# A hybrid decoder layer on one core: two groups' raw weights loaded ahead of conditioning rows, a list of thresholds for the visits, and another offset for the first parts

## The chip, the cores and the metric

The kernel runs on one core of one Trainium2 chip. The metric is the time on the device in microseconds (us); lower is better. Times given as a median come from runs without a profile; the views come from one profiled execution, which has a time of its own. TensorE multiplies matrices, VectorE and ScalarE work on elements, GpSimd is hardly used, and SyncE (SP) issues most transfers.

## The reference

One decoder layer over 256 tokens of width 2048, all in fp32. A conditioning vector c gives six vectors of 2048 values by one large product, and the first two scale and shift the normalized input. The first large product, h W_in, feeds a retention branch and an HGRN2 branch; a gated feed-forward part follows.

```python
mod = jax.nn.silu(c) @ w_ada[l] + b_ada[l]
shift1, scale1, gate1, shift2, scale2, gate2 = jnp.split(mod, 6, axis=-1)

h = modulate(rms_norm(x, g_norm1[l]), shift1, scale1)
p = h @ w_in[l]
rq, rk, rv, rg, hq, hf, hi, hg, ga, gb = jnp.split(p, split_at, axis=-1)
...
x = x + gate1[:, None, :] * (merged @ w_out[l])
h2 = modulate(rms_norm(x, g_norm2[l]), shift2, scale2)
u = causal_depthwise_conv(h2 @ w_up[l], conv_w[l], conv_b[l])
a, bgl = jnp.split(u, 2, axis=-1)
x = x + gate2[:, None, :] * ((jax.nn.silu(a) * bgl) @ w_down[l])
return rms_norm(x, g_final)
```

## The kernel before

**Products in three parts.** A product in fp32 is made of three products in a faster format: every weight and every activation is split into an upper part (rounded) and a lower part (the rest), and upper x upper, upper x lower and lower x upper are summed. For a piece of weights, `load` (line 158) brings 128 partitions x up to two k tiles x 512 columns by the SP queue into one of eleven buffers called raw; `upper` (line 169) makes the upper part wh on ScalarE (line 176); `rest` (line 179) makes the lower part wl on VectorE (line 181). `pieces` (line 185) hands out such pieces one after the other. wh and wl have four buffers each, with 64 spare elements; `part` (line 164) places the part at an offset in bytes given by `shift`, a pair for wh and wl. `COLS` is (8, 8), the default is (0, 0).

**The stage that the change touches.** It multiplies h by twelve column groups of W_in (`ATT`), each 512 columns wide, over sixteen k tiles of 128 rows. Groups are counted from 0, so the sixth and seventh are groups 5 and 6. Groups 0 to 3 give their output turned (`mm_cols`, twelve matmuls of 256 columns a k tile, lines 221, 222 and 225), groups 4 to 11 in rows (`mm_rows`, six matmuls of 512 columns a k tile, lines 205, 206 and 210). In the column groups the weights are the stationary operand.

A k tile of h needs its own scale and shift, that is two dot products of c's silu with two rows of w_ada a k tile. Each row comes in two loads, and VectorE multiplies and sums each of the four (`ada_dot`, line 507); ScalarE turns the sums into scale and shift (lines 518, 519 and 524) and makes h's upper part and h itself (lines 434 and 435), and VectorE h's lower part (line 436). So the k tiles of h come one after the other, and the stage works on those that are there. Rows of w_ada and pieces of weights share the raw buffers and the SP queue.

The first two k tiles are worked off by hand for groups 0 to 3 (lines 899 to 948), in an order that is kept as written (`pin`). Line 949 prepares the first piece of group 4 (`FIRST`), lines 950 and 951 start the conditioning of the third k tile: its first two loads and products. From line 952 on the order on an engine is the scheduler's, which places instructions by the order of the program and by when it expects their inputs.

**Visits.** `visits` (line 971) plans the rest: it goes round the groups, and at each visit a group takes all k tiles that have come into use since its last one. `work` counts the k tiles done over all groups and begins at 8; the number of k tiles in use is have = min(16, 2 + int((work - LAG) / ADA_EVERY)), with LAG 2 and ADA_EVERY 11. A visit finishes the conditioning that it needs (line 1003), multiplies into a PSUM bank (`products`), prepares the next visit's first piece (`early`, line 986) and then adds the bank to the group's sum in SBUF (`take`, line 876: a copy on ScalarE, line 880, at a group's first visit; an add on VectorE, line 882, later). The banks called pg are two, so a visit starts when the take of the visit two before is done; groups 0 and 1 stay in banks of their own until the end. After each piece `pump` lets the conditioning go on by a share of `pace`, about 0.73 a pair of k tiles where one of its steps counts 1.15.

The plan has 56 visits and 105 pieces. Its first visits are, as (group, k tiles): (4, 2), (5, 2), (6, 2), (7, 3), (8, 3), (9, 3), (10, 3), (11, 4), (0, 2), (1, 2), (2, 2), (3, 3); the last are (5, 3), (6, 3), (7, 2), (8, 2), (9, 2), (10, 1), (11, 1). Behind the groups follow the keys of the retention, the gates, the two output products, the up projection and the down projection, which the change does not touch. Groups 0, 2 and 4, when complete, start the HGRN2 work of four heads (`hgrn`, line 610), whose element-wise steps fill VectorE and ScalarE beside the products.

Of the kernel before, what the change touches and what calls it, by code (L numbers as in the profile page):

```python
# [23 lines left out]
KT = D // P  # L24
# [5 lines left out]
G = 512  # L30
NORM_EPS = 1e-6
HEAD_EPS = 1e-5
FIRST = 4
RESIDENT = 2
ADA_EVERY = 11
LAG = 2
NOSYNC = mybir.DependencyInfo(mybir.DependencyClass.NoSync, mybir.DependencyReason.DATA)
SMALL = 70
COLS = (8, 8)
# [21 lines left out]
class Kernel:  # L61
# [104 lines left out]
        full = self.wp.tile([P, 2 * G + 64], F32R, name=f"{name}_{self.n}", tag=name, bufs=4)  # L166
        return full[:, shift // 4 : shift // 4 + m * w].rearrange("p (m w) -> p m w", m=m)

    def upper(self, src, m, w, gain=None, shift=(0, 0)):

        raw = self.load(src, m, w)
        if gain is not None:
            self.pin(self.nc.vector.tensor_tensor(raw, raw, gain[:, None, :].to_broadcast([P, m, w]), ALU.mult))
        self.n += 1
        wh, wl = [self.part(n, m, w, at) for n, at in zip(("wh", "wl"), shift)]
        self.pin(self.nc.scalar.activation(wh, raw, AF.Copy))  # L176
        return raw, wh, wl
# [4 lines left out]
        self.pin(self.last)  # L182
        return wh, wl

    def pieces(self, src, kts, gain=None, shift=(0, 0)):

        uppers = []
        for k in range(0, kts, 2):
            m = min(2, kts - k)

            while len(uppers) <= k // 2 + (gain is not None) and 2 * len(uppers) < kts:
                at = 2 * len(uppers)
                z = min(2, kts - at)
                uppers.append(self.upper(src[:, at : at + z, :], z, G, gain, shift))
            wh, wl = self.rest(uppers[k // 2])
            uppers[k // 2] = None
            yield [(k + j, wh[:, j, :], wl[:, j, :]) for j in range(m)]
# [35 lines left out]
    def mm_apart(self, pss, pieces, act):  # L233

        nc = self.nc
        n = range(len(pss))
        for pick, cols in ((0, slice(0, T)), (0, slice(T, 2 * T)), (1, slice(0, T))):
            for i in n:
                for j in range(4):
                    out = pss[i][j // 2][:, j % 2 * T : (j % 2 + 1) * T]  # L240
                    w = pieces[i][pick][:, 0, j * P : (j + 1) * P]
                    self.pin(nc.tensor.matmul(out, lhsT=w, rhs=act[:, cols], start=False, stop=False, skip_group_check=True))
# [17 lines left out]
    def wide_group(self, src, act):  # L260

        nc = self.nc
        pgs = [self.pg(), self.pg()]
        ps = pgs[0][:2] + pgs[1][:2]
        steps = list(range(0, KT, 4))
        pieces = self.pieces(src, KT, shift=WIDE)
        for k in steps:
            items = [(act(kt), wh, wl) for _ in range(2) for kt, wh, wl in next(pieces)]
            for pair in (0, 2):
                self.mm_wide(ps, items, k == 0, k == steps[-1], pair)  # L270
                self.pump()
        out = self.blk([P, 4, T], name="p")
        for pair in (0, 2):
            dst = out[:, pair : pair + 2, :]
            z = pgs[pair // 2][2]
            nc.scalar.activation(dst, z[:, :, T:], AF.Copy)
            nc.vector.tensor_tensor(dst, dst, z[:, :, :T], ALU.add)
        return out
# [567 lines left out]
    def run(self):  # L846
        nc, a = self.nc, self.a
# [11 lines left out]
        def act(k):  # L859
            return hT[k // 2][:, k % 2, :]  # L860
# [32 lines left out]
        def opening(k):  # L893

            z = self.s1([P, T], name="z")
            self.pin(nc.scalar.activation(z, self.xT[0][:, k, :], AF.Identity, bias=self.dots[:, 0:1], scale=s1[:, k : k + 1]))
            return z
# [10 lines left out]
        z = opening(0)  # L908
# [9 lines left out]
        uppers = []  # L918
        for g in range(RESIDENT, FIRST):
            if g == RESIDENT:  # L920
                self.pin(nc.scalar.activation(hi, h, AF.Copy))
            uppers.append(self.upper(a["wa"][g][:, 0:1, :], 1, G))
        self.pin(nc.vector.tensor_tensor(lo, h, hi.bitcast(F32), ALU.subtract))
        rests = [self.rest(z) for z in uppers]
        self.times(1, 1, rx_sb)
# [3 lines left out]
        for g in range(RESIDENT, FIRST):  # L929
            ps[g] = self.pg()  # L930
            wh, wl = rests[g - RESIDENT]
# [3 lines left out]
        z = opening(1)  # L935
        for _ in gen:
            pass
        uppers = [self.upper(a["wa"][g][:, 1:2, :], 1, G) for g in range(RESIDENT)]
        hi, lo = act(1)[:, :T], act(1)[:, T:]
        summed(hi, z, self.dots)  # L940
        h = self.s1([P, T], name="h")
# [2 lines left out]
        rests = [self.rest(z) for z in uppers]  # L944
        self.mm_apart([ps[g] for g in range(RESIDENT)], rests, act(1))
        for g in range(RESIDENT, FIRST):
            wh, wl = self.rest(self.upper(a["wa"][g][:, 1:2, :], 1, G))
            mms[g](ps[g], [(act(1), wh[:, 0, :], wl[:, 0, :])], False, True)
        begun = list(self.pieces(a["wa"][FIRST][:, 0:2, :], 2))
        for _ in range(2):  # L950
            next(ada[2])
        self.ordered = False
# [9 lines left out]
        def visit(g):  # L962
            return COLS if g in cols else (0, 0)
# [6 lines left out]
        def visits():  # L970
            work, g = sum(done), FIRST
            seen = list(done)
            while min(seen) < KT:
                have = min(KT, 2 + int((work - LAG) / ADA_EVERY))
                m = have - seen[g]
                if m > 0:
                    yield g, m, work
                    seen[g] = have
                    work += m
                else:  # L980
                    work += 0.5
                g = (g + 1) % len(ATT)
                if have == KT and seen[0] < KT:
                    g = min(i for i in range(len(ATT)) if seen[i] < KT)

        def early(g, m):
            k = done[g]
            pieces = self.pieces(a["wa"][g][:, k : k + m, :], m, shift=visit(g))
            return chain([next(pieces)], pieces)

        small = False
        plan = list(visits())
        for g in range(RESIDENT, FIRST):
            take(g, ps[g], True)
        for n, (g, m, work) in enumerate(plan):
            if work > SMALL and not small:
                small = True
                self.small_loads(nc.sync, ("freq", "lbT", "lmask"))
                self.start(self.trig())
                self.start(self.lower_bound())  # L1000
            fresh = done[g] == 0
            have = done[g] + m
            self.finish(*ada[:have])
            bank = ps[g] if g < RESIDENT else self.pg()
            whole = g >= RESIDENT
            self.products(mms[g], bank, a["wa"][g], act, done[g], m, first=whole, last=whole or have == KT, shift=visit(g), begun=begun)
            done[g] = have
            begun = early(*plan[n + 1][:2]) if n + 1 < len(plan) else None
            if whole or have == KT:
                take(g, bank, fresh or not whole)  # L1010
            if have == KT and ATT[g] in GATES:
                nc.scalar.activation(accs[g], accs[g], AF.Silu)
                gates[GATES.index(ATT[g])] = accs[g]
            for hb in range(2):
                gs = [hb, 2 + hb, 4 + hb]
                if g in gs and min(done[i] for i in gs) == KT:
                    self.pace(0, 14.0, 24)
                    begin(self.hgrn, hb, *(accs[i] for i in gs))
                    for i in gs:
                        accs[i] = None  # L1020
# [63 lines left out]
        for j in range(4):  # L1084
            last = j == 3
            x1.append(self.load_rows(j))
            if not last:
                g = self.row(self.gate["gate1"], j, "g1")
            if j == 2:
                g3 = self.row(self.gate["gate1"], 3, "g1")  # L1090
            elif last:
                g = g3
            ps = self.products(self.mm_rows, self.po2() if last else self.pg(), a["wout"][j], actm, 0, KT, hold=4 * last, gain=g if last else None)
            if last:
                g = None
# [302 lines left out]
```

## Time and profile before

| what | us |
|---|---|
| median of 3 runs (1504.5 to 1504.94) | 1504.68 |
| the profiled execution | 1503.57 |
| its span, first to last instruction | 1501.8 |
| TensorE busy in the span | 1485.5 |
| VectorE busy | 1210.5 |
| ScalarE busy | 839.8 |

The views count from the start of the span. A row of a timeline has the start, the length, the engine (PE is TensorE, PEld its weight loads, DVE VectorE, ACT ScalarE, SPq the SP queue), the line of the kernel, the operation, the tiles as output<-inputs, the shape and a count; in brackets stands how long the engine was idle before it and what ended that. Rows of alike instructions without a gap are merged. A matmul of 512 columns is shown 0.39 long while the next starts 0.23 later, since matmuls overlap in the array. In a view by windows each row has the window, its length, the busy time of PE, PEld, DVE, ACT and POOL with counts, the granted TensorE clock, the DMA engines' mean share and GB/s. The granted clock is 1.00 in all windows after the first 20 us.

### The profile page before, as it was taken

How to read it: one execution, taken by the hardware profiler on the slowest of the kernel's cores; microseconds unless marked ns; L12 is line 12 of the kernel's file. 1: busy time of each engine (PE TensorE's matmuls, PEld its weight loads, DVE VectorE, ACT ScalarE, POOL GpSimd, SP SyncE). 2: the span in 40 equal slices, each digit the busy share in tenths (PEclk: the TensorE clock that was granted, in tenths of full speed). 3: DMA queues.
4: the chain of work that ended last, by engine and by line, in shares of the span. 5: the costliest groups of instructions: out<-in, count | busy, mean ns of one | idle time of the engine just before them, and what ended most of it. 6: DMA issues, size and time to landing. Idle time of an engine off the chain costs nothing.

```text
span 1501.8 us, 22826 instructions
## 1 busy us (share of the span) xinstructions
PE 1485.5 (99%) x8537; PEld 1274.6 (85%) x8537; DVE 1210.5 (81%) x1654; ACT 839.8 (56%) x1211; POOL 4.0 (0%) x8
## 2 busy tenths in 40 slices
PE   8999999999999999999999999999999999999997
PEld 7888889888888888888888888888888888888886
DVE  7899997999999877898978778778777769455694
ACT  5645546867775644445466555555555558344342
POOL 0000000000000000000000000000000000000000
PEclk9999999999999999999999999999999999999999
DMA  9999997688887889989847777777777666666551
GB/s 371 370 308 350 350 324 262 210 290 279 278 284 263 281 298 325 312 293 363 306 132 241 249 232 234 233 235 237 232 245 234 221 188 208 195 210 212 178 185 56
DMA packets 111455, 385.73 MB, mean 257 GB/s; under 512 B 12864, under 2 KB 13424, under 8 KB 111344
## 3 DMA queue, kind: packets, MB, share of 16 engines
q1 hardware_dynamic: 110448, 383.14, 76.3%
q8 instruction: 67, 1.10, 0.3%
q10 hardware_dynamic: 896, 1.13, 0.2%
q14 instruction: 44, 0.36, 0.1%
HBM read 382.11 MB, written 2.11 MB: 256 GB/s over the span
## 4 chain that ended last, share of the span: by engine, by line
PE 90%; DVE 5%; ACT 2%; DMA 1%; issue 1%; DVEq 0%; ACTq 0%; SPq 0%
PE pg L205 12%; PE pg L210 12%; PE pg L206 12%; PE po L1231 11%; PE pg L1231 11%; PE po L1233 5%; PE pg L1233 5%; PE pg L255 4%; PE po L206 3%; PE po L205 3%; PE po L210 3%; DVE wl L181 2%; PE pg L258 2%; DVE raw L507 1%; DVE p L882 1%
## 5 line engine op out<-in xcount | busy, mean ns | idle before, releaser
L181 DVE TENSOR_TENSOR wl<-raw,wh 128x1024 fp32r<-128x1024 f32 (+1 forms) x535 | 631.2, 1190 | 225.4 <-ACT wh L176 217.2
L176 ACT ACTIVATE wh<-raw 128x1024 fp32r<-128x1024 f32 (+1 forms) x535 | 545.8, 1032 | 468.1 <-PE pg L206 185.2
L507 DVE SCALAR_TENSOR_TENSOR raw<-raw,sc 128x1024 f32<-128x1024 f32 (+2 forms) x194 | 233.5, 1209 | 0.0
L205 PE MATMUL pg<-wh,hT 128*128 128x512 f32 x512 | 202.4, 396 | 3.7 <-ACT wh L176 2.6
L206 PE MATMUL pg<-wh,hT 128*128 128x512 f32 x512 | 199.8, 390 | 0.0
L1231 PE MATMUL po<-h2T,wh 128*128 128x512 f32 x704 | 175.8, 392 | 0.0
L1231 PE MATMUL pg<-h2T,wh 128*128 128x512 f32 x688 | 172.1, 392 | 0.0
L1231 PEld LDWEIGHTS po<-h2T,wh 128*128 128x128 f32 x704 | 125.7, 188 | 21.7
L1231 PEld LDWEIGHTS pg<-h2T,wh 128*128 128x128 f32 x688 | 122.8, 188 | 21.2
L210 PE MATMUL pg<-wl,hT 128*128 128x512 f32 x512 | 138.9, 390 | 0.3 <-DVE wl L181 0.3
L205 PEld LDWEIGHTS pg<-wh,hT 128*128 128x128 f32 x512 | 96.1, 188 | 25.3 <-ACT wh L176 4.9
L210 PEld LDWEIGHTS pg<-wl,hT 128*128 128x128 f32 x512 | 95.9, 188 | 21.0 <-DVE wl L181 0.9
L206 PEld LDWEIGHTS pg<-wh,hT 128*128 128x128 f32 x512 | 96.2, 188 | 19.4 <-DVE hT L436 0.3
L1233 PEld LDWEIGHTS po<-h2T,wl 128*128 128x128 f32 x704 | 93.4, 188 | 7.5
L1233 PEld LDWEIGHTS pg<-h2T,wl 128*128 128x128 f32 x688 | 91.3, 188 | 7.3
L1233 PE MATMUL po<-h2T,wl 128*128 128x256 f32 x704 | 94.5, 277 | 0.0
L1233 PE MATMUL pg<-h2T,wl 128*128 128x256 f32 x688 | 92.5, 277 | 0.0
L206 PE MATMUL pg<-wh,gs 128*128 128x512 f32 x176 | 68.6, 390 | 0.0
L205 PE MATMUL pg<-wh,gs 128*128 128x512 f32 x176 | 68.5, 389 | 0.0
L205 PE MATMUL po<-wh,gs 128*128 128x512 f32 x176 | 68.5, 389 | 0.0
L206 PE MATMUL po<-wh,gs 128*128 128x512 f32 x176 | 68.5, 389 | 0.0
L1244 ACT ACTIVATE u<-uy,convw 128x256 f32<-128x256 f32 x88 | 52.4, 595 | 28.7 <-DVE uy L1242 28.4
(273 smaller groups left out, 2033.9 us busy)
## 6 DMA issues: line engine op xcount, KB each, us to landing
raw<-in_wup SPq DMA_DIRECT2D x176, 512.0 KB, 4.5
raw<-in_wdown SPq DMA_DIRECT2D x88, 512.0 KB, 4.1
raw<-in_wa SPq DMA_DIRECT2D x79, 512.0 KB, 5.5
raw<-in_ada SPq DMA_DIRECT2D x64, 512.0 KB, 5.6
raw<-in_wab SPq DMA_DIRECT2D x64, 512.0 KB, 5.2
raw<-in_ada SPq DMA_DIRECT2D x62, 512.5 KB, 5.6
raw<-in_gate SPq DMA_DIRECT2D x32, 512.5 KB, 4.8
raw<-in_wk SPq DMA_DIRECT2D x32, 512.0 KB, 4.9
```

The lines of the kernel that those rows point to most:

```text
L176: self.pin(self.nc.scalar.activation(wh, raw, AF.Copy))
L181: self.last = self.nc.vector.tensor_tensor(wl, raw, wh.bitcast(F32), ALU.subtract)
L205: nc.tensor.matmul(ps[t], lhsT=act[:, hi], rhs=wh, start=first and i == 0, stop=False)
L206: nc.tensor.matmul(ps[t], lhsT=act[:, lo], rhs=wh, start=False, stop=False)
L210: nc.tensor.matmul(ps[t], lhsT=act[:, hi], rhs=wl, start=False, stop=last and i == len(items) - 1)
L255: nc.tensor.matmul(ps[z], lhsT=wh[:, z * P : (z + 1) * P], rhs=act, start=first and i == 0, stop=False)
L258: nc.tensor.matmul(ps[z][:, :T], lhsT=wl[:, z * P : (z + 1) * P], rhs=act[:, :T], start=False, stop=last and i == len(items) - 1)
L507: dot = self.pin(nc.vector.scalar_tensor_tensor(raw[:, 0, :], raw[:, 0, :], 1.0, self.sc[:, at:to], ALU.mult, ALU.mult, accum_out=part[:, ...
L882: nc.vector.tensor_tensor(dst, dst, z, ALU.add)
L1231: self.pin(nc.tensor.matmul(ps[z], lhsT=wh[:, z * P : (z + 1) * P], rhs=act, start=kt == 0, stop=False, skip_group_check=bool(begun)))
L1233: nc.tensor.matmul(ps[z][:, :T], lhsT=wl[:, z * P : (z + 1) * P], rhs=act[:, :T], start=False, stop=kt == KT - 1, skip_group_check=bool(be ...
L1244: nc.scalar.activation(u, y, AF.Identity, bias=w[3], scale=w[2])
```

## The change

Three things change. The first parts of the two k tiles that are done by hand lie at offset 8 for groups 0 to 3. The raw weights of groups 5 and 6 for their first visit are loaded right behind group 4's and ahead of the third k tile's conditioning; `early` passes them on instead of loading them. And have is counted from a list, `READY`, of values of work at which another k tile comes into use: 14, 24, 34, 45, 56 and so on to 155, where the old rule gave 13, 24, 35, 46, 57 to 156.

```diff
-LAG = 2
+READY = (14, 24, 34, *range(45, 156, 11))
...
-    def upper(self, src, m, w, gain=None, shift=(0, 0)):
+    def upper(self, src, m, w, gain=None, shift=(0, 0), raw=None):
 
-        raw = self.load(src, m, w)
+        raw = raw or self.load(src, m, w)
...
-    def pieces(self, src, kts, gain=None, shift=(0, 0)):
+    def pieces(self, src, kts, gain=None, shift=(0, 0), raw=None):
...
-                uppers.append(self.upper(src[:, at : at + z, :], z, G, gain, shift))
+                uppers.append(self.upper(src[:, at : at + z, :], z, G, gain, shift, raw if at == 0 else None))
...
-            uppers.append(self.upper(a["wa"][g][:, 0:1, :], 1, G))
+            uppers.append(self.upper(a["wa"][g][:, 0:1, :], 1, G, shift=COLS))
...
-        uppers = [self.upper(a["wa"][g][:, 1:2, :], 1, G) for g in range(RESIDENT)]
+        uppers = [self.upper(a["wa"][g][:, 1:2, :], 1, G, shift=COLS) for g in range(RESIDENT)]
...
-            wh, wl = self.rest(self.upper(a["wa"][g][:, 1:2, :], 1, G))
+            wh, wl = self.rest(self.upper(a["wa"][g][:, 1:2, :], 1, G, shift=COLS))
             mms[g](ps[g], [(act(1), wh[:, 0, :], wl[:, 0, :])], False, True)
         begun = list(self.pieces(a["wa"][FIRST][:, 0:2, :], 2))
+        stock = {g: self.load(a["wa"][g][:, 0:2, :], 2, G) for g in range(FIRST + 1, FIRST + 3)}
         for _ in range(2):
             next(ada[2])
...
-                have = min(KT, 2 + int((work - LAG) / ADA_EVERY))
+                have = 2 + sum(work >= at for at in READY)
...
-            pieces = self.pieces(a["wa"][g][:, k : k + m, :], m, shift=visit(g))
+            pieces = self.pieces(a["wa"][g][:, k : k + m, :], m, shift=visit(g), raw=stock.pop(g, None))
```

With the list the plan has 54 visits and 104 pieces. It is the old one up to the visit (1, 2) at work 32; then come (2, 3), (3, 3), (4, 3), (5, 3), (6, 4), (7, 3), (8, 3), (9, 4), and the last are (4, 3), (5, 2), (6, 2), (7, 1), (8, 1), (9, 1), (11, 5).

## The prediction

> **What bounds the kernel now.** The profile's page comes first: TensorE is busy 99% of the span, VectorE 81%. A TensorE that hardly stops can be made faster only where it waits, so the next view is the list of TensorE's waits between 28 and 310 us, the stage with the visits that the change touches. Its columns: total us, times, longest.
>
> ```profile
> span 1501.8 us, 22826 instructions
> PE 1485.5 (99%) x8537; PEld 1274.6 (85%) x8537; DVE 1210.5 (81%) x1654; ACT 839.8 (56%) x1211; POOL 4.0 (0%) x8
> PE pg L205 <- ACT wh L176: 2.6, 2, 2.1
> PE pg L205 <- DVE p L882: 1.0, 2, 0.6
> PE pg L210 <- DVE wl L181: 0.3, 1, 0.3
> ```
>
> All that can be won in the stage is these 3.9 us and the slow restart behind each wait. The largest, 2.06 us, stands before group 5 (the sixth). The timelines of TensorE, ScalarE and the sync queue show why (start, length, engine, line).
>
> ```profile
> 33.35 1.07 PE L210 MATMUL pg<-wl,hT 128*128 128x512 f32 x4
> 36.48 0.50 PE L205 MATMUL pg<-wh,hT 128*128 128x512 f32 x1 [2.06 <-ACT wh L176]
> 38.43 1.07 PE L210 MATMUL pg<-wl,hT 128*128 128x512 f32 x4
> 39.33 0.39 PE L205 MATMUL pg<-wh,hT 128*128 128x512 f32 x1
> 42.05 0.39 PE L205 MATMUL pg<-wh,hT 128*128 128x512 f32 x1
> ...
> 32.94 0.30 ACT L518 ACTIVATE s<-dot 128x1 f32<-128x1 f32 x1 [0.20 <-DVE raw L507]
> 33.27 0.39 ACT L519 ACTIVATE s<-gn,s 128x1 f32<-128x1 f32 x1
> 34.46 1.02 ACT L880 ACTIVATE p<-pg 128x1024 f32<-128x1024 f32 x1 [0.80 <-PE pg L210]
> 35.38 2.00 ACT L176 ACTIVATE wh<-raw 128x1024 fp32r<-128x1024 f32 x2
> ...
> 22.41 1.64 SPq L161 DMA_DIRECT2D raw<-in_ada  x3
> 24.40 0.33 SPq L161 DMA_DIRECT2D raw<-in_wa  x1
> 25.02 0.33 SPq L161 DMA_DIRECT2D raw<-in_ada  x1
> 25.70 0.33 SPq L161 DMA_DIRECT2D raw<-in_wa  x1
> ```
>
> Group 5's raw weights are the transfer issued at 24.40, behind three conditioning rows. ScalarE makes its upper part (L176, two conversions in 2.00 us) only after it has emptied group 4's bank (L880), which waits for group 4's last matmul. The list of DMA issues, asked for one issue at a time, gives the landing (last column: us from issue): the first row of the three, then group 5, then group 6 (issued at 25.70).
>
> ```profile
> raw<-in_ada SPq DMA_DIRECT2D x1, 512.0 KB, 6.5
> ...
> raw<-in_wa SPq DMA_DIRECT2D x1, 512.0 KB, 8.3
> ...
> raw<-in_wa SPq DMA_DIRECT2D x1, 512.0 KB, 9.5
> ```
>
> They land at 28.9, 32.7 and 35.2: (35.2 - 28.9) / 5 = 1.26 us for each 512 KB place in the queue, in the order of issue. The queue, not the issuing, sets these landings.
>
> **Part 1, the raw weights of groups 5 and 6 first.** No instruction is added. Two loads move on the sync queue past four conditioning rows, two that are issued before the visits and two from their first steps. Groups 5 and 6 take the first two of six places, landing at 28.9 and 30.2; the four rows land at 31.4, 32.7, 34.0 and 35.2. From the seventh place on every landing stays, because the bytes ahead of it are the same. ScalarE can convert group 5 (1.0 us) between 29 and 31, before L880 needs it at 34.4. Group 5 then follows group 4 as group 6 follows group 5, whose last lower matmuls start 39.33 - 38.43 = 0.90 ahead of it: start 33.35 + 0.90 = 34.25, end 34.25 + 2.72 = 36.97 (42.05 - 39.33 = 2.72 a pair of k tiles). Against 39.33 that is **2.36 us**, all on the path.
>
> What is late next? The delayed rows feed hT of the third k tile, whose first use, in group 7, is one pair after 42.05, at 44.77; it moves to 42.4.
>
> ```profile
> L507 DVE SCALAR_TENSOR_TENSOR raw<-raw,sc 128x1024 f32<-128x1024 f32 (+2 forms) x194 | 233.5, 1209 | 0.0
> L181 DVE TENSOR_TENSOR wl<-raw,wh 128x1024 fp32r<-128x1024 f32 x67 | 80.7, 1220 | 9.4 <-ACT wh L176 9.4
> 43.82 0.42 DVE L436 TENSOR_TENSOR hT<-h,hT 128x256 fp32r<-128x256 f32 x1
> ```
>
> From the first row's landing at 31.4, VectorE has four products and two lower parts of 1.22 each, and waits a little for landings: the last product ends near 38.8. The four short steps behind it (L524, L434, L435, L436), at 0.5 each by L518's 0.30 and L436's 0.42, end near 40.8: hidden, with 1.6 us to spare; with that cover gone a late row costs its lateness one for one. The lower part of group 5, even behind two products, ends near 35.2 and is needed at 34.25 + 1.95 (38.43 - 36.48) = 36.2. Group 7's own weights (seventh place, 36.5) are needed at 39.7, two conversions later. All are covered.
>
> **Part 2, first parts at offset 8.** It changes addresses alone. The column groups show both offsets: twelve matmuls of one k tile at offset 0, then at 8.
>
> ```profile
> 28.63 0.28 PE L221 MATMUL pg<-hT,wh 128*128 128x256 f32 x1
> 30.07 0.28 PE L221 MATMUL pg<-hT,wh 128*128 128x256 f32 x1
> ...
> 243.86 0.28 PE L221 MATMUL po<-hT,wh 128*128 128x256 f32 x1
> 245.25 0.28 PE L221 MATMUL po<-hT,wh 128*128 128x256 f32 x1
> ...
> 25.69 2.14 PE L242 MATMUL po<-hT,wh 128*128 128x256 f32 x16 [0.78 <-ACT wh L176]
> ```
>
> 1.44 against 1.39 us. Six k tiles are so moved; two lie ahead of the wait at 25.69, which swallows them, four run in one chain from there into group 4: 4 x 0.05 = **0.20 us**. The Trainium skill, TensorE: Matmul & The Clock Gate, Back-to-back issue gap, gives the gap of a warm 256-column matmul by its column count alone (N/2.4 + 2.5, 109 ns); by it this part is worth nothing and the sum below 2.3 instead of 2.5. The trace's 120 and 116 ns speak against that, though no row shows one group at both offsets.
>
> **Part 3, the list.** By the old rule a new k tile comes in at work 13, 24, 35, 46 ... 156, by the new list at 14, 24, 34, 45 ... 155. Followed through the loop of visits, nothing differs until work 34; there group 2 takes three k tiles instead of two, and so on: 54 visits instead of 56, 104 weight pieces instead of 105. TensorE's matmuls stay the same. VectorE is at 10.00 of 10 us from near 100 us on (first row, fifth number), and its steps are the takes (L882) and lower parts (L181) besides the products:
>
> ```profile
> 100.00:110.00 10.00, 9.44 (x42) 7.33 (x41) 10.00 (x14) 5.38 (x10) 0.00 (x0) 1.00 0.97 322
> 104.69 0.50 PE L205 MATMUL pg<-wh,hT 128*128 128x512 f32 x1 [0.56 <-ACT wh L176]
> 117.94 0.42 DVE L436 TENSOR_TENSOR hT<-h,hT 128x256 fp32r<-128x256 f32 x1
> 122.38 0.28 PE L221 MATMUL pg<-hT,wh 128*128 128x256 f32 x1
> 145.02 0.42 ACT L572 ACTIVATE n<-ang 128x256 f32<-128x256 f32 x1 [3.88 <-DVE ang L571]
> 270.97 2.31 DVE L636 TENSOR_TENSOR_SCAN b<-ones,f 128x128 f32<-128x128 f32 x7
> 274.46 1.21 DVE L882 TENSOR_TENSOR p<-p,pg 128x1024 f32<-128x1024 f32 x1
> 275.59 3.49 DVE L181 TENSOR_TENSOR wl<-raw,wh 128x1024 fp32r<-128x1024 f32 x3
> 280.12 0.68 DVE L181 TENSOR_TENSOR wl<-raw,wh 128x512 fp32r<-128x512 f32 x1
> 280.73 0.68 DVE L649 TENSOR_TENSOR qe<-qe,q 128x512 f32<-128x512 f32 x1
> 280.35 0.47 PE L205 MATMUL pg<-wh,hT 128*128 128x512 f32 x1 [0.58 <-DVE p L882]
> ```
>
> The stop at 104.69 falls where the seventh k tile comes into use. A matmul is 0.39 long and starts 0.23 behind the one before (2.72 / 12), so a recorded wait moves the starts by 0.16 more: 0.72. Counted as the program traces it, the new plan has one take (1.21) and one single lower part (0.68) less ahead of that hT, and needs it one k tile (1.36) earlier: 0.5 us more room, so I take **0.5** of 0.72 as gone; the bounds are none and all. The eighth k tile loses room: three single lower parts less (2.0), needed three k tiles (4.1) sooner. Its hT was done at 118.4 and its pair began at 122.38, so of four us two stay. Later k tiles have as much room or more, as fewer takes lie ahead. The angles' chain, which stops ScalarE for 3.88 us ahead of 145.02 and delays weights by a recorded 0.25 on TensorE, I leave as it is, between 0.4 won and as much lost.
>
> The end of the stage gets harder. The last visits were 3, 3, 2, 2, 2, 1, 1 k tiles; now they are 2, 2, 1, 1, 1, 5. Two banks alternate, so a visit starts when the take of the visit two before is done. Before, the two stops there (1.0 in the list of waits, 0.16 more each) cost 1.3. A single-k visit holds TensorE 1.36 and VectorE 1.13 (274.46 to 275.59) + 0.61 (280.12 to 280.73) = 1.74; one filler like L649 adds 0.60. Behind a prompt take, done 1.3 after its visit, the next two takes end at 3.04 and 4.78 without fillers, at 3.64 and 5.98 with them, where TensorE wants them by 2.7 and 4.1: 0.7 to 1.9 us lost. I take 1.9, since the rows show VectorE filling such places with other work: **-0.6** against before. The Trainium skill, Perfetto Trace Analysis, Matmuls, has groups rotate through PSUM banks so that the evacuation of one overlaps the next group's matmuls; by it the tail costs no more and the sum is 3.1. The wait at 280.35 shows two banks not covering it here.
>
> **Sum:** 2.36 + 0.20 + 0.50 - 0.60 = 2.46. The profiled execution took 1503.57 (the span's 1501.8 and 1.8 around it); the runs' median is 1504.68, 1.1 more. With 2.5 off, the profile comes near 1501.1, its span near 1499.3, and the median at **1502.2**. A difference of 0.2% (3.0 us) is about what a measurement tells from no change.
>
> **Rivals.** (a) Every other wait goes too: 2.36 + 0.20 + 0.72 = 3.3, with 0.4 near 150 and 1.2 of the end's 1.3 up to 4.9; middle 4.1: 1500.6. For it: fewer takes; against: VectorE at 10.00. (b) The wait forms anew: ScalarE keeps L518 and L519 ahead of group 5's L176. The second row now lands at 32.7, its product ends at 33.9, L519 at 34.6, L176 at 35.6 instead of 36.4: 0.8 won, the 0.20 hidden in it: 1503.9. For it: that is the old order; against: the weights land 2.5 us ahead of the row. (c) Slower: scans (2.31) instead of L649 fall before the takes of the single visits. With a filler f before each of three takes the last ends at 4.78 + 3f where 4.1 is wanted; at f = 2.31 that loses 7.6, less the 1.3 of before and the 3.06 won: +3.2, 1507.9. It turns the sign from f = 1.23 on. Against: the scans came ahead of these visits so far. (d) The change doesn't do what it says: group 5's L176 stays behind L880 though its weights are there, and 36.48 stays: 1504.7.
>
> **Chances.** Forecast 0.50 (1501.1 to 1503.5), (a) 0.22, (b) 0.15, (c) 0.07, (d) 0.06. The range 1499.8 to 1504.7 runs from (a)'s end to (d) and leaves out (c) and odd cases. Below 1501.67 lie most of (a) and three tenths of the forecast: faster 0.35; above 1507.69 half of (c): slower 0.04; the rest, 0.61, lies within 0.2%.
>
> **What would show it.** Right: no wait before group 5, its L176 ahead of L880 and near 29 to 31, group 6 starting near 36.8, the opening's L221 at 0.116, and waits on L882 at the single visits of 1 to 2 us in all. Wrong: L518 between the landing and L176; hT of the third k tile after 42.4; TensorE stopping where the fifth or eighth k tile comes in; a stage that ends no earlier although it began 2.5 us ahead.

## The result and the profile after

The changed kernel is slower: 1513.36 us in the median (1511.93 to 1513.54, four runs) against 1504.63 (1504.5 to 1504.94, four runs) in the same session. The ratio is 1.0056 with a 95% interval of 1.0038 to 1.0073. The profiled execution took 1513.45. The forecast of 1502.2, its range and its direction were wrong. Most of its signs of being right came all the same: no wait before group 5, the conversion of group 5 ahead of group 4's copy (at 31.82, a little late), L221 at 0.116, waits of 1.1 us on L882. So did signs of being wrong: hT of the third k tile is done at 44.0, after 42.4; TensorE stops for 0.4 us where the fifth k tile comes in (75.02, the L436 in the list below); and the stage ends later.

The page of the changed kernel, and TensorE's waits between 28 and 400 us (total us, times, longest):

```profile
span 1511.7 us, 22801 instructions
PE 1489.2 (99%) x8537; PEld 1278.6 (85%) x8537; DVE 1209.0 (80%) x1651; ACT 836.8 (55%) x1207; POOL 4.0 (0%) x8
PE pg L255 <- DVE p L277: 4.7, 1, 4.7
PE pg L205 <- ACT wh L176: 3.0, 2, 2.1
PE po L221 <- ACT wh L176: 1.1, 1, 1.1
PE pg L205 <- DVE p L882: 1.1, 2, 0.6
PE pg L222 <- DVE hT L436: 0.4, 1, 0.4
PE pg L205 <- ACT hT L434: 0.2, 1, 0.2
```

The wait of 2.06 on L176 is still in the list, and a wait of 4.7 has come that was 0.3 before. It stands on line 277, in the wide groups (the retention's keys), which the change does not touch. Where the 9.88 us of span arose is seen by cutting both traces at the starts of the same matmuls. The table does so for all traces of this study; its rows below "changed" are the experiments that follow. The columns are us between: the start and group 4; groups 4 and 5; groups 5 and 7; group 7 and the visit of group 0 (the eighth); that visit and the first wide group (first L255); there and the last L255; the rest.

| kernel | to 4 | 4 to 5 | 5 to 7 | 7 to 0 | 0 to wide | wide | rest | span |
|---|---|---|---|---|---|---|---|---|
| before | 31.51 | 4.97 | 5.57 | 21.76 | 225.54 | 97.35 | 1115.08 | 1501.78 |
| changed | 32.09 | 2.73 | 7.66 | 23.54 | 227.58 | 103.31 | 1114.75 | 1511.66 |
| list alone (e1) | 31.62 | 4.97 | 7.18 | 21.76 | 226.86 | 104.29 | 1114.63 | 1511.31 |
| loads alone (e2) | 31.18 | 2.74 | 7.67 | 23.48 | 226.03 | 97.33 | 1114.99 | 1503.42 |
| offset alone (e3) | 30.93 | 4.97 | 5.58 | 21.76 | 225.55 | 97.36 | 1115.01 | 1501.16 |
| changed, step back (e4) | 31.04 | 2.72 | 7.66 | 23.51 | 227.57 | 97.35 | 1115.11 | 1504.96 |
| before, step less (e5) | 31.25 | 4.97 | 7.20 | 21.77 | 225.21 | 100.53 | 1114.62 | 1505.55 |
| list, step back (e6) | 31.29 | 4.97 | 7.17 | 21.76 | 226.86 | 97.34 | 1115.04 | 1504.43 |
| three groups, offset (e7) | 30.79 | 2.72 | 5.44 | 22.66 | 226.61 | 97.36 | 1115.10 | 1500.68 |
| four groups, offset (e8) | 31.27 | 2.73 | 5.44 | 22.66 | 225.96 | 97.37 | 1115.04 | 1500.47 |
| before, late step (e9) | 31.18 | 4.96 | 5.58 | 21.76 | 225.53 | 97.38 | 1115.08 | 1501.47 |
| e8 with late step (e10) | 32.66 | 2.73 | 5.44 | 22.65 | 225.98 | 97.36 | 1115.04 | 1501.86 |
| list, four groups, offset, step back (e11) | 31.76 | 2.75 | 5.44 | 22.64 | 226.89 | 97.35 | 1115.00 | 1501.83 |

The first column differs by a microsecond and more between runs whatever was changed (30.79 to 32.66), so the 0.58 there can't be put down to the change. One execution of e3 took 3861.04 us; e3's ratio leaves it out. The rest of the loss has four places: the 2.24 won before group 5 are lost again before group 7 (-2.24, +2.09); 1.78 behind group 7; 2.04 in the visits; 5.96 in the wide groups.

**Group 7.** TensorE and ScalarE of the changed kernel around groups 5 to 7, and the landing of group 7's weights, issued at 27.72 (last column of its row: us to landing):

```profile
34.82 0.39 PE L205 MATMUL pg<-wh,hT 128*128 128x512 f32 x1
37.54 0.39 PE L205 MATMUL pg<-wh,hT 128*128 128x512 f32 x1
42.48 0.50 PE L205 MATMUL pg<-wh,hT 128*128 128x512 f32 x1 [2.06 <-ACT wh L176]
```

```profile
31.82 1.05 ACT L176 ACTIVATE wh<-raw 128x1024 fp32r<-128x1024 f32 x1
...
33.68 1.05 ACT L176 ACTIVATE wh<-raw 128x1024 fp32r<-128x1024 f32 x1
...
37.74 1.03 ACT L880 ACTIVATE p<-pg 128x1024 f32<-128x1024 f32 x1 [1.69 <-PE pg L210]
38.66 0.28 ACT L518 ACTIVATE s<-dot 128x1 f32<-128x1 f32 x1
...
40.46 1.02 ACT L880 ACTIVATE p<-pg 128x1024 f32<-128x1024 f32 x1 [0.28 <-PE pg L210]
41.38 1.05 ACT L176 ACTIVATE wh<-raw 128x1024 fp32r<-128x1024 f32 x1
```

```profile
raw<-in_wa SPq DMA_DIRECT2D x1, 512.0 KB, 8.7
```

Groups 5 and 6 are converted at 31.82 and 33.68, and group 5 follows group 4 without a stop. Group 7's weights are there at 27.72 + 8.7 = 36.4. ScalarE is idle for 1.69 us up to 37.74, but its next instruction is the copy of group 5's bank. The conversion that TensorE wants stands behind group 6's copy at 40.46, which itself waits for group 6's last matmul. In the program it is traced ahead of that copy (`early` stands before `take`); the scheduler's order has put it behind. It is the picture that before shows at group 5, two groups later.

**The wide groups.** TensorE at the seam between the third and the fourth wide group; first before, then the changed kernel with ScalarE and VectorE:

```profile
359.41 0.39 PE L765 MATMUL po<-p,a 128*128 128x128 f32 x2
359.56 2.09 PE L255 MATMUL pg<-hT,wh 128*128 128x512 f32 x8
...
362.42 1.99 PE L255 MATMUL pg<-hT,wh 128*128 128x512 f32 x8
...
365.66 0.74 PE L255 MATMUL pg<-hT,wh 128*128 128x512 f32 x2 [0.32 <-DVE p L277]
```

```profile
369.18 0.39 PE L765 MATMUL po<-p,a 128*128 128x128 f32 x2
374.31 1.12 PE L255 MATMUL pg<-hT,wh 128*128 128x512 f32 x3 [4.74 <-DVE p L277]
```

```profile
371.50 0.28 ACT L769 ACTIVATE sqh<-po 128x128 f32<-128x128 f32 x1
...
372.60 0.59 ACT L276 ACTIVATE p<-pg 128x512 f32<-128x512 f32 x1
373.08 0.30 ACT L353 ACTIVATE rsh<-ssh,eps 128x4 f32<-128x4 f32 x1
373.27 0.60 ACT L276 ACTIVATE p<-pg 128x512 f32<-128x512 f32 x1
```

```profile
372.14 1.13 DVE L773 SCALAR_TENSOR_TENSOR oh<-po,rsh,p 128x128 f32<-128x128 f32 x4
...
373.51 0.66 DVE L277 TENSOR_TENSOR p<-p,pg 128x512 f32<-128x512 f32 x1
374.08 1.12 DVE L773 SCALAR_TENSOR_TENSOR oh<-po,rsh,p 128x128 f32<-128x128 f32 x4
375.12 0.68 DVE L277 TENSOR_TENSOR p<-p,pg 128x512 f32<-128x512 f32 x1
```

A wide group fills both pg banks and empties them by line 276 (ScalarE) and line 277 (VectorE); the next wide group can't start before. HGRN2 steps are traced by `pump` behind each pair of a wide group's matmuls. The step with L765 is the end of four HGRN2 heads: squares (L769), a square root's table (L353) and products (L773). Before, two more rounds of L255 and L258, 5.5 us of TensorE, lie between it and the group's end. In the changed kernel it is the last thing traced ahead of L276, and its squares and products stand before the emptying on both engines, so that L276 comes 3.0 us behind L765's end (372.60 - 369.57) and 4.8 us behind the group's own last matmul (367.79). Of the 5.96 us, 4.42 are the longer wait (4.74 against 0.32). Behind it TensorE ran for one window at a granted clock of 0.50, which fits the other 1.5:

```profile
374.90:378.31 3.41, 3.41 (x12) 2.84 (x11) 0.89 (x3) 3.37 (x6) 0.95 (x1) 0.50 0.44 177
```

Why it is later follows from the code. Behind group 5's last visit `pump` gives 14/24 = 0.583 of credit a pair of k tiles and half of it for a single one. The old plan has pairs and singles worth 5.5 pairs from there, the new one 5.0. Counted step by step, the credit at the end stands at +0.21 in the old plan, by which one more step (line 629's Sqrt, price 3.3) was taken, and at -0.08 in the new. Then the credit is reset, and the missing step moves everything behind it.

### The profile page after: what moved, and what is told of

The parts are those of the page before. It is cut to its first block, busy times and chain, and to the rows that moved or that the text cites. A ratio compares the mean times of both kernels' runs of the same rounds, so it can differ in the third digit from the quotient of the medians.

```text
span 1511.7 us, 22801 instructions
## 1 busy us (share of the span) xinstructions
PE 1489.2 (99%) x8537; PEld 1278.6 (85%) x8537; DVE 1209.0 (80%) x1651; ACT 836.8 (55%) x1207; POOL 4.0 (0%) x8
## 4 chain that ended last, share of the span: by engine, by line
PE 93%; DVE 3%; ACT 1%; DMA 1%; issue 1%; DVEq 0%; ACTq 0%
PE pg L205 13%; PE pg L210 13%; PE pg L206 13%; PE po L1232 11%; PE pg L1232 10%; PE po L1234 5%; PE pg L1234 5%; PE pg L255 4%; PE po L210 3%; PE po L205 3%; PE po L206 3%; PE pg L258 2%; DVE raw L507 1%; DVE wl L181 1%; DMA raw<-in_wa 1%
## 5 line engine op out<-in xcount | busy, mean ns | idle before, releaser
L176 ACT ACTIVATE wh<-raw 128x1024 fp32r<-128x1024 f32 (+1 forms) x534 | 546.1, 1034 | 471.0 <-PE pg L206 192.2
L255 PE MATMUL pg<-hT,wh 128*128 128x512 f32 x256 | 66.0, 401 | 4.7 <-DVE p L277 4.7
```

The source lines that it names most:

```text
L255: nc.tensor.matmul(ps[z], lhsT=wh[:, z * P : (z + 1) * P], rhs=act, start=first and i == 0, stop=False)
```

## The experiments

The theory behind the changed kernel's time, after this reading, has three parts. "Moved wait": ScalarE's order puts the first conversion whose weights come behind the rows after the copy of the bank before it, so the wait moves with the number of groups loaded ahead. "Seam": the list costs one HGRN2 step, whose output then falls on the end of the third wide group. "Visits": the list has a price inside the visits. Against "seam" stands "loads": the later HGRN2 work and line 277 suffer from the moved transfers. Each ratio is against the kernel before on the same chip in the same session, with its 95% interval.

**e1, the list alone**

```diff
-LAG = 2
+READY = (14, 24, 34, *range(45, 156, 11))
...
-                have = min(KT, 2 + int((work - LAG) / ADA_EVERY))
+                have = 2 + sum(work >= at for at in READY)
```

> The new list alone: no loads ahead, first parts at offset 0. Theory 'seam' (the list ends the visits with one step of the HGRN2 work fewer traced, so that the heads' output falls on the end of a wide group of the retention's keys and holds up the emptying of both banks): about +6 to +8 us against before, with a wait of 4 to 5 us of TensorE on L277 near 370 us; the wait of 2.06 us before group 5 stays. Rival 'loads' (the delay comes from the conditioning rows being put behind the loads): within 1.5 us of before.

Measured: 1512.31 us, ratio 1.0050 (1.0033 to 1.0067). Its waits:

```profile
PE pg L255 <- DVE p L277: 4.8, 1, 4.8
PE pg L205 <- ACT wh L176: 3.0, 2, 2.1
```

Nearly the whole loss is the list's: the wait on L277 is here without any moved load, and "loads" falls as the cause of it. Group 5's wait is the old one.

**e2, the loads alone**

```diff
+        stock = {g: self.load(a["wa"][g][:, 0:2, :], 2, G) for g in range(FIRST + 1, FIRST + 3)}
```

with `raw` handed through `early`, `pieces` and `upper` as in the change.

> The loads of groups 5 and 6 ahead, alone: old rule of the visits, offset 0. Theory 'moved wait': groups 5 and 6 start without a wait, and the same 2.06 us stands before group 7, whose upper part is placed behind group 6's take on ScalarE: -0.5 to +2 us against before, the upper end if the granted clock is halved for 3.4 us behind that wait. Rival 'loads' (the delayed conditioning rows are what made the change slower): +5 us or more.

Measured: 1505.29, ratio 1.0010 (1.0000 to 1.0019). Group 5 starts 2.74 behind group 4, and the wait stands before group 7 (7.67 from group 5 to group 7 where two pairs take 5.44). The loads by themselves win nothing; the interval reaches 1.0000, so that they lose is not certain. The stretch from group 7 to the visit of group 0 is 1.72 longer, since the granted clock falls behind the moved wait (below).

**e3, the offset alone**

```diff
-            uppers.append(self.upper(a["wa"][g][:, 0:1, :], 1, G))
+            uppers.append(self.upper(a["wa"][g][:, 0:1, :], 1, G, shift=COLS))
```

and the same for the two other places of the first parts.

> The first parts at offset 8, alone. If a matmul with stationary weights at offset 8 is 4 ns shorter: -0.2 us, which is within what can be told from no change; L221 in the opening at 0.116 instead of 0.120 us. If the place of the weights does nothing: 0, and L221 at 0.120.

Measured: 1503.53, ratio 0.9994 (0.9985 to 1.0004), not to be told from no change. The trace shows the term itself. TensorE of this run, then the same start of group 4 in the kernel before:

```profile
25.29 2.10 PE L242 MATMUL po<-hT,wh 128*128 128x256 f32 x16 [0.46 <-ACT wh L176]
...
30.93 0.40 PE L205 MATMUL pg<-wh,hT 128*128 128x512 f32 x1
```

```profile
31.51 0.40 PE L205 MATMUL pg<-wh,hT 128*128 128x512 f32 x1
```

From L242's start to group 4 it is 30.93 - 25.29 = 5.64 against 31.51 - 25.69 = 5.82: 0.18 won. The same stretch takes 5.63 to 5.67 in all seven traces with the offset and 5.82 or 5.83 in all six without it, and the column groups' matmuls there start 0.116 apart with it and 0.120 without.

**e4, the changed kernel with one HGRN2 step more**

```diff
+        self.turn(0)
         self.xT = None
```

> The whole change, and one more step of the HGRN2 work traced at the end of the visits, so that its later steps stand where they stood before. Theory 'seam': the wait on L277 near 370 us goes, and with it the halved clock behind it: about 6 us faster than the change, 1507 to 1508. Rival 'visits' (the list loses in the visits themselves, by conditioning that is needed earlier): no more than 1 us faster than the change, 1512 to 1513.

Measured: 1506.58, ratio 1.0012 (1.0002 to 1.0021), a little under the 1507 to 1508 of "seam". One step traced behind the last visit takes the wait on L277 back to 0.3:

```profile
PE pg L255 <- DVE p L277: 0.3, 1, 0.3
```

The wide groups take 97.35 again instead of 103.31. By the ratios, 1.0056 and 1.0012, that step is worth 0.44%, 6.6 of the 8.7 us. What is left is group 7's wait and the 2.0 us in the visits.

**e5, the kernel before with one step less**

```diff
+            if n + 1 == len(plan):
+                self.rate[0] = 0.0
             self.products(mms[g], bank, a["wa"][g], act, done[g], m, first=whole, last=whole or have == KT, shift=visit(g), begun=begun)
```

> The kernel before with one thing changed: at the last visit the pump gives queue 0 no credit, so that two HGRN2 steps instead of three are traced between the completion of the last group and the wide groups; list, loads and offset are the old ones. Theory 'seam' (the loss of 7 to 8 us comes from the HGRN2 work standing one step later when the wide groups begin, whatever causes that): the wait before L255 on L277 grows from 0.3 to 4 to 5 us near 370, and the time is 1509 to 1512. Rival 'list' (the late L277 comes from the list's other order of weights and takes): no wait above 1 us there, 1504 to 1506.

Measured: 1506.62, ratio 1.0016 (1.0006 to 1.0025). TensorE at the same seam:

```profile
365.16 0.39 PE L765 MATMUL po<-p,a 128*128 128x128 f32 x2
368.43 1.19 PE L255 MATMUL pg<-hT,wh 128*128 128x512 f32 x2 [2.88 <-DVE p L277]
```

The wait forms with the old list, so the step is a cause by itself and the list isn't needed for it. But it is 2.9 long instead of the 4 to 5 expected, and 1506.62 lies between the two ranges. ScalarE has fewer squares left ahead of L276 here (one at 366.03, then L276 at 366.28) than in the changed kernel (four from 371.12 on). Why the order of the two differs so, with the same step missing, wasn't tried. Its expectation counts two steps for three; by the credit it is three for four behind group 5's last visit.

**e6, the list with the step back**: e1 and e4's added line.

> The new list alone and one more HGRN2 step at the end of the visits; loads and offset are the old ones, so group 5's wait of 2.06 stays. Theory 'seam' with 'visits' (the list has a price of its own inside the visits, by the stops near 74, 105 and 126 that the changed kernel shows and the old one doesn't): no wait above 1 us on L277, the wide groups start 1.3 to 2.0 us later than before, time 1505.5 to 1506.8. Rival 'free list' (those stops come from the loads or the offset): 1504 to 1505. Rival 'no seam' (the step does not matter with the list alone): the wait of 4.7 stays, 1512.

Measured: 1505.97, ratio 1.0010 (1.0001 to 1.0019). The wait on L277 is 0.3 again, and there are 226.86 in the visits where before has 225.54: the list costs 1.32 us in the visits by itself. "Free list" and "no seam" fall.

**e7, three groups' raw weights ahead, old list, offset 8**

```diff
+        stock = {g: self.load(a["wa"][g][:, 0:2, :], 2, G) for g in range(FIRST + 1, FIRST + 4)}
```

> The old list, the first parts at offset 8, and the raw weights of groups 5, 6 and 7 ahead of the rows instead of two groups. Theory 'moved wait' (the wait stands before the first group whose weights come behind the rows, because ScalarE's order puts its L176 behind the take of the group before): no wait before groups 5, 6 and 7, group 7 starts near 39.2 instead of 42.05; what is late next is hT of the third k tile, whose rows land 1.26 later still, done at 42.3 to 43.4 where 41.9 is wanted: 0.4 to 1.5 of the 2.7 us given back, the time 1502.0 to 1503.3. Rival 'wait stays' (a wait of 2 us forms anew at the next piece, of group 7's third k tile or of group 8): 1503.5 to 1505.3.

Measured: 1503.09, ratio 0.9992 (0.9982 to 1.0001). ScalarE, then TensorE:

```profile
31.47 1.02 ACT L880 ACTIVATE p<-pg 128x1024 f32<-128x1024 f32 x1
32.38 2.00 ACT L176 ACTIVATE wh<-raw 128x1024 fp32r<-128x1024 f32 x2
34.27 1.02 ACT L880 ACTIVATE p<-pg 128x1024 f32<-128x1024 f32 x1
```

```profile
42.44 0.50 PE L205 MATMUL pg<-wh,hT 128*128 128x512 f32 x1 [0.61 <-ACT wh L176]
```

With group 7's weights loaded ahead, its conversion (the second of the two at 32.38) moves in front of the copies of groups 4 to 6, and groups 4 to 7 run without a stop: 2.72 and 5.44. What comes late next is not hT, which is done at 42.3, the early end of the expected 42.3 to 43.4, but the upper part of the third k tile's own piece, which ScalarE makes behind L434 and L435: 0.61. The time falls into the range of "moved wait", though the interval still touches no change.

**e8, four groups ahead**: as e7, with `FIRST + 5`.

> As the run with three groups loaded ahead, with group 8's raw weights too. Theory 'moved wait': the weights of group 8 have margins above 2 us already, so nothing is won by them, and the third k tile's rows land another 1.26 us later: hT at 43.5 to 44.7 where 41.9 is wanted, 0.8 to 1.3 us slower than with three groups: 1503 to 1504.5. Rival 'wait stays': if with three groups a wait forms before group 8, it is gone here and the time is 1 to 2 us under that run.

Measured: 1502.22, ratio 0.9987 (0.9977 to 0.9996). The expected loss against three groups did not come. Up to the visit of group 0 the two traces agree (22.66 behind group 7 in both), so the load of group 8 neither hurts nor helps there. They differ by 0.65 in the visits, where e7 has a stop of 1.67 from start to start near 102 and e8 one of 1.19. By their ratios the two can't be told apart.

**e9, the kernel before with the step behind the visits**: e5's two lines and e4's one.

> The kernel before, with the last HGRN2 step of the visits taken out of the last visit and traced right behind the visits instead; nothing else. The run without that step (old list) started the second wide group 2.0 us earlier, measured from the visits' eighth, because the two stops before the last visits (0.97 and 0.85 from start to start) were gone, and lost 4.9 at the seam. Theory 'seam' (what counts at the seam is how many steps have been traced when the wide groups begin, not in which visit): the wait on L277 stays 0.3, and the 2.0 us, or a part of them, are kept: 1502.0 to 1503.5 where the kernel before gives 1503.9 to 1504.6. Rival 'the step costs the same wherever it stands': within 0.5 of the kernel before. Rival 'phase' (any shift of that step brings the wait): 1506 to 1511.

Measured: 1504.71, ratio 1.0000 (0.9991 to 1.0008). The wait on L277 stays 0.3, so the number of steps counts and not the visit in which the last is traced. The hoped-for 2.0 did not come either: the rival "the step costs the same wherever it stands" holds. The two stops before the last visits are here again, 0.98 and 0.84 from start to start. e5 lacked them because it left the step out, not because the last visit was free of it.

**e10, e8 with the late step**

> Old list, first parts at offset 8, four groups' raw weights ahead of the rows, and the late HGRN2 step. If the two gains add up (1.7 by the run with four groups, 0.5 to 2.0 by the late step): 1500.3 to 1502.0, ratio 0.9975 to 0.9990. If the earlier opening brings a new order of the HGRN2 steps at the wide groups: a wait above 1 us on L277 and 1503 or more.

Measured: 1503.03, ratio 0.9987 (0.9978 to 0.9996): e8's gain and nothing more, as e9 says. The time lies above the range for added gains; the ratio lies inside, but that range holds e8's own 0.9987.

**e11, the changed kernel with four groups ahead and the step back**

> The changed kernel with the list kept, four groups' raw weights ahead instead of two, and one HGRN2 step more at the end of the visits: the two repairs together. Theories 'moved wait' and 'seam' with 'visits': no wait above 1 us before groups 5 to 8 and none on L277, so that only the list's own price is left, 1.3 to 2.1 us against the run with four groups and the old list (1502.2): 1503.5 to 1504.3, in its trace stops near 103 and 125 of 1.2 to 1.5 from start to start. Rival 'free list': 1501.7 to 1502.7. Rival 'a third cause': above 1505.

Measured: 1503.49, ratio 0.9989 (0.9979 to 0.9999), just under the range for "moved wait", "seam" and "visits" together. Both large waits are gone. In the visits it has 226.89 against e8's 225.96: beside the other repairs the list costs 0.93. By their ratios the two kernels can't be told apart, so this price stands on the traces alone.

## Why the prediction was wrong

**Part 1.** The landings came as worked out (36.4 for group 7, 36.5 predicted), and group 5 followed group 4 at once: 2.24 of the 2.36. Its conversion came at 31.82 and not between 29 and 31: ScalarE sat idle for 1.71 us up to 30.90, with the weights there, and then copied group 2's bank first. That cost TensorE nothing, but it is the same order already. The step that failed is "Group 7's own weights (seventh place, 36.5) are needed at 39.7, two conversions later. All are covered." It compares a landing with a need and leaves out where the conversion stands on ScalarE. The profile before had shown that a conversion stands behind the copy of the bank before it; I used that for group 5 only. Rival (d) had this mechanism, at the wrong group. e7 and e8 show it from the other side. The delayed third k tile, which I had weighed at length, was not the limit.

**The price of a wait.** The sum took a wait at its length and 0.16. Behind the moved wait 1.78 more were lost, about 1.6 of them by the granted clock, which is in none of my terms, because before had the same wait without it. Two views by windows show the difference; the columns are window, length, busy time of PE, PEld, DVE, ACT, POOL, the granted clock, DMA share and GB/s. First before, then the changed kernel:

```profile
31.27:34.69 3.42, 3.15 (x16) 2.31 (x14) 2.79 (x6) 1.98 (x5) 0.00 (x0) 1.00 1.02 406
34.69:38.10 3.41, 1.62 (x7) 1.36 (x8) 1.64 (x2) 2.68 (x3) 0.00 (x0) 1.00 1.03 413
```

```profile
40.39:43.81 3.42, 1.36 (x7) 1.09 (x7) 1.35 (x2) 3.35 (x5) 0.00 (x0) 1.00 1.03 405
43.81:47.22 3.41, 3.41 (x10) 2.64 (x9) 3.41 (x6) 1.07 (x2) 0.00 (x0) 0.50 0.95 323
```

In before the wait is shared by two windows and the clock stays at 1.00. In the changed kernel it falls into one, and in the window behind it TensorE starts 10 matmuls instead of the 17 that it has in such a window at full clock: 7 x 0.23 = 1.6.

**Part 2.** Right: 0.20 predicted, 0.18 measured. The formula of the Trainium skill (TensorE: Matmul & The Clock Gate, Back-to-back issue gap) goes by the column count alone, and by it nothing was to be won; it does not hold for this pair of offsets, which measured 0.120 and 0.116. The section gives it for an isolated matmul and says that in a stream the weight loads count too. Why the offset counts is not shown here.

**Part 3, in the visits.** Predicted +0.50 at the seventh k tile and -0.60 at the end; measured -1.32 in all (e6). At the seventh k tile the stop did not shrink but doubled. At the eighth the count of hT held: it was done at 120.84, and its first pair began at 121.86, without a stop. But a stop came one group later, in the same k tile's second pair. TensorE at both places, and ScalarE ahead of each:

```profile
105.95 0.50 PE L205 MATMUL pg<-wh,hT 128*128 128x512 f32 x1 [0.25 <-ACT hT L434]
107.39 0.50 PE L205 MATMUL pg<-wh,hT 128*128 128x512 f32 x1 [0.94 <-ACT wh L176]
...
128.68 0.39 PE L221 MATMUL po<-hT,wh 128*128 128x256 f32 x1 [1.10 <-ACT wh L176]
```

```profile
104.97 0.30 ACT L524 ACTIVATE t<-dot 128x1 f32<-128x1 f32 x1 [4.89 <-DVE raw L507]
...
106.30 1.99 ACT L176 ACTIVATE wh<-raw 128x1024 fp32r<-128x1024 f32 x2
...
125.44 0.29 ACT L518 ACTIVATE s<-dot 128x1 f32<-128x1 f32 x1 [3.37 <-DVE raw L507]
...
126.17 1.28 ACT L587 ACT_TABLE_LOAD   x1
127.46 0.22 ACT L587 ACTIVATE lbe<-lbe 128x16 f32<-128x16 f32 x1
127.58 1.04 ACT L176 ACTIVATE wh<-raw 128x1024 fp32r<-128x1024 f32 x1
```

I had counted VectorE's work ahead of hT. At these two places TensorE waited for hT itself for only 0.25 us; the rest was weights. ScalarE stood 4.89 us at L524 and 3.37 us at L518 for VectorE's product, and the conversions were behind that: at the first place behind L434 and L435 too, at the second behind L587's table load of 1.28. That is the mechanism of group 7 once more. The row at 104.69 in the prediction already names L176. The end of the stage, priced at 0.60 by VectorE's fillers, cost about the same as before, where -0.60 was forecast: stops of 0.45 and 0.64 in the list of waits against 0.58 and 0.46.

**What no step looked at.** The second step that failed is the end of Part 3: the sum's +0.50 - 0.60 for the list follows it to the end of the visits and no further, and so puts everything behind them at nothing. The prediction names the HGRN2 steps only as fillers of VectorE; that their number depends on the pieces that the list removes, and that the rest goes on in the wide groups, is not in it. These 6 us are the largest part of the loss. Rival (c) had the right sign with another mechanism.

The version that beats the kernel before is the one with the old list, the offset and four groups loaded ahead (e8): 0.9987 (0.9977 to 0.9996), about 2 us by the ratio. Its trace shows 1.2 of them: 2.37 won from group 4 to group 7 and 0.18 by the offset, less 0.90 lost up to the visit of group 0 and 0.42 in the visits. The rest would fit executions of the kernel before in which its wait halves the clock (last section), since its times spread from 1502.97 to 1506.52 and e8's from 1502.07 to 1503.20; no trace of such an execution was taken, so this is not shown.

## What to carry to other kernels

A load that arrives earlier helps only if the instruction that uses it also moves on its in-order engine; find that place for the group behind the last one helped, since the wait goes there. An edit that removes pieces also removes the slots in which background work is traced: follow the background work into the next stages and see whether one of its steps now falls between a group's last matmul and the emptying of its banks. A short wait has two prices, and which one applies is decided by a clock window, so compare traces, not single times.

## What the runs showed of the hardware

The granted clock changes in a grid of 3.41 us that is not tied to the start of the program: in the kernel before, e1 and e5, which are alike up to there, a window starts at 34.69, 33.86 and 33.72, that is 3.18, 2.24 and 2.47 behind group 4's start. The clock falls to 0.50 behind a window in which TensorE was busy for too small a share, even if not idle. In the thirteen traces, from 20 us on and up to 400, every window at full clock with 1.36 us of busy TensorE or less (nine of them: 0.00 to 0.72 three times, 1.35 or 1.36 six times) was followed by one at 0.50; every window with 1.50 or more (from 1.50, 1.62 and 1.62 up) was followed by 1.00. The same wait of 2.06 us leaves 1.36 where it falls into one window, as in e1, and 1.62 or more where two share it, as in the kernel before:

```profile
33.86:37.27 3.41, 1.35 (x6) 0.80 (x6) 0.86 (x3) 2.71 (x3) 0.00 (x0) 1.00 1.03 413
37.27:40.68 3.41, 3.41 (x10) 2.64 (x9) 2.80 (x4) 0.51 (x2) 0.00 (x0) 0.50 1.03 406
```

So the same code has two lengths by the phase of that grid alone: from group 5 to group 7 it takes 5.57 in the kernel before and 7.20 in e5, about 1.6 us more. The Trainium skill (TensorE: Matmul & The Clock Gate, What's actually happening) has a free-running window of 3413 ns, and the traces agree with that length. It lists the half clock behind an idle window; here 2.05 of 3.41 us without work were enough.
